# Attention of a decoder trunk on one core: the next queries' rotation before the normalising, one sum and reciprocal for a pair of heads, and low parts of outputs and late weights on GpSimd

## The chip, the cores and the metric

One NeuronCore of a Trainium2 chip runs the whole kernel. The metric is the time of one execution on the device in microseconds (us); before the change the median of three runs is 1023.88 us. Engines are named as in the profile: PE is TensorE (matrix products and transposes), DVE is VectorE, ACT is ScalarE, POOL is GpSimd, SP is SyncE, which issues loads.

## The reference, cut to what matters

A residual stream of 512 tokens and 1024 channels passes a gated convolution layer with its feed-forward layer, and then a layer of sliding-window attention with its feed-forward layer. The change touches only the attention: 16 query heads of 64 channels, 4 shared key and value heads, blocks of 128 queries that see their own and the previous 128 keys, and one learned sink per head that takes part in the softmax.

```
q = partial_rotary((rmsnorm(h) @ w_q).reshape(s, 16, 64))
scores = einsum(q, k) / 8, masked to the last 128 keys
probs = softmax(concatenate([scores, sink]))[..., :-1]
attn = einsum(probs, v) @ w_o
h = h + rmsnorm(attn)
```

## The kernel before, in words

All products are in float32 made of two parts: a tile is rounded to a high part (on ACT, `AF.Copy` into an fp32r tile) and the rest, value minus high part, is its low part (a `tensor_tensor` subtract, mostly on DVE). Three matmuls, high by low, high by high and low by high, make one product (`mm3`, L193 to L195 of the profile).

The attention handles eight pairs of heads, t = 0 to 7. It is written as rounds i = 0 to 9 of a loop, and the string `ORDER` says in which order the steps of a round are recorded; every engine then works through its own instructions in just that order. A letter is a step, a digit its part, and a minus at its end means the pair before. In round i:

- `R-` rotates the queries of pair i+1: DVE shuffles the PSUM tile `pq` into `sh` (L1261) and multiplies `pq` by the cosines into `ra` (L1263); POOL multiplies `sh` by the sines (L1267) and adds it to `ra` (L1270). Once L1263 has read it, the PSUM bank of `pq` is free again.
- `S0 S1` are the scores of pair i on PE (L1334, tiles `psc`). For the rounds in `NEXT` (0 to 4, 6 and 7) `S1` is moved right behind `S0`, and then its banks come from the four that `pq` also uses.
- `M0 M1` are mask and maxima on DVE (L1346), `E00` to `E11` the exponentials on ACT (L1362) with the sink's own exponential after each half (L1369). Half 0 is query blocks 0 and 1, half 1 is blocks 2 and 3.
- `N0 N1` normalise on DVE: for each half an addition of sums and sink (L1374), a reciprocal (L1376), and four multiplications of the exponentials (L1379, tiles `s`).
- `T0` to `T3` transpose the probabilities of pair i-1 on PE (L1391, tiles `pt`), `P` and `L` make their high and low parts (L1404 on ACT, L1408 on DVE), `W` multiplies them by the values (L1417, tiles `po`).
- `O-` joins the two halves of `po` of pair i-2 (L1426 on ACT, L1428 on DVE), `o-` splits the result into high and low part (L1436 on ACT, L1437 on DVE). The output products read these: those of pairs 0 to 3 (`Z`, `z`, tiles `pe`) from round 5 on, those of pairs 4 to 7 (tiles `pmix`) behind the loop.
- `Q0` to `Q3` project the queries of pair i+2 on PE into `pq`; `G` loads and splits the weights of pair i+3, and in rounds 5 to 8 the late output weights `rest_w` (L182 on ACT, L183 on DVE); `g` does so for the early ones; `H-` splits the rotated queries of pair i+1 (L1280 on ACT, L1281 on POOL).

Beside that the loop issues transfers on POOL's queue that add weight blocks in memory for the second feed-forward layer (L547). They are released at the ends of rounds by `sum_on`; `R-` issues half of those that wait and `H-` the rest. In the trace a round is best counted from the first instruction of `M0` on DVE, the only place where L1346 has 128 columns; rounds 1 to 5 begin at 557.8, 569.7, 583.7, 596.8 and 612.7 us.

Of the kernel before, what the change touches and what calls it, by code (L numbers as in the profile page):

```python
# [44 lines left out]

EARLY_IN, REST_IN = 2, 0
ORDER = (
    "R- S0 T0 T1 O- Q0 M0 Q1 o- Z0 P0 P1 S1 T2 T3 L0 Q2 L1 G M1 E00 E01 k H- g0 Q3 P2 P3 E10 E11 Z1 z0 W0 L2 L3 A A A N0 W1 W2 N1 W3 g1 z1"
)
NEXT = (0, 1, 2, 3, 4, 6, 7)  # L50
STEP = {
# [6 lines left out]
EARLY = 4  # L58
# [16 lines left out]
def yoco_kernel(  # L75
# [22 lines left out]
    nc = tc.nc  # L98
# [7 lines left out]
    small = ctx.enter_context(tc.tile_pool(name="small", bufs=3))  # L106
# [7 lines left out]
    def name(s):  # L114
        uid[0] += 1
        return f"{s}_{uid[0]}"
# [55 lines left out]
            h = at[1].start // S  # L172
            return self.of[h][:, at[1].start - h * S : at[1].stop - h * S]

    def split_weights(src, raw=None, slots=False):
        if raw is None:
            raw = fetch(src)
        if slots:
            hi, lo = Two("whi", F32R), Two("wlo", F32R)
            for h in range(2):  # L180
                c = slice(h * S, (h + 1) * S)
                nc.scalar.activation(hi[:, c], raw[:, c], AF.Copy)  # L182
                nc.vector.tensor_tensor(out=lo[:, c], in0=raw[:, c], in1=hi[:, c].bitcast(F32),  # L183
                                        op=ALU.subtract)
            return hi, lo
        hi = wsp.tile([P, D], F32R, tag="whi", name=name("whi"))
        lo = wsp.tile([P, D], F32R, tag="wlo", name=name("wlo"))
        nc.scalar.activation(hi, raw, AF.Copy)
        nc.vector.tensor_tensor(out=lo, in0=raw, in1=hi.bitcast(F32), op=ALU.subtract)
        return hi, lo  # L190
# [366 lines left out]
    for l in range(2):  # L557
# [3 lines left out]
        for rd, (f0, f1) in enumerate(ROUNDS[:-1]):  # L561
            k = slice(f0 // 2, f1 // 2)
# [744 lines left out]
    class Heads:  # L1307
# [44 lines left out]

        def exponents(self, half, i):
            pe, nm = self.pe[half], self.nm[half]
            if i == 0:
                se = small.tile([P, 2, 2], F32, tag="se", name=name("se"))
                rs = small.tile([P, 2, 2], F32, tag="rs", name=name("rs"))
                self.sums[half] = se, rs
            se, rs = self.sums[half]
            cc = self.spans(half)[i][1]  # L1360
            for e in range(2):
                nc.scalar.activation(  # L1362
                    pe[e][:, cc], pe[e][:, cc], AF.Exp, bias=nm[:, e, i : i + 1],
                    scale=-1.0, accum_out=rs[:, e, i : i + 1],
                )
            if i == 1:
                for e in range(2):
                    h = 2 * self.t + e
                    nc.scalar.activation(se[:, e], nm[:, e], AF.Exp, bias=snk[:, h : h + 1])  # L1369

        def normalise(self, half):
            se, rs = self.sums[half]
            pe = self.pe[half]
            nc.vector.tensor_tensor(out=se, in0=se, in1=rs, op=ALU.add)  # L1374
            rd = small.tile([P, 2, 2], F32, tag="rd", name=name("rd"))
            nc.vector.reciprocal(out=rd, in_=se)  # L1376
            for i, cc in self.spans(half):
                for e in range(2):
                    nc.vector.tensor_scalar(  # L1379
                        out=pe[e][:, cc], in0=pe[e][:, cc], scalar1=rd[:, e, i : i + 1],  # L1380
                        scalar2=None, op0=ALU.mult,
                    )
# [48 lines left out]
        def out(self):  # L1431
            if self.t < BOTH:
                hi, lo = halves("ohl", F32R)
            else:
                hi, lo = slot("ohi", F32R), slot("olo", F32R)
            nc.scalar.activation(hi, self.o, AF.Copy)  # L1436
            nc.vector.tensor_tensor(out=lo, in0=self.o, in1=hi.bitcast(F32), op=ALU.subtract)  # L1437
            at.append((hi, lo))

    class Early:  # L1440
# [17 lines left out]
    early_w, rest_w = [], []  # L1458
# [5 lines left out]
    with tc.manual_schedule(engines=ALL):  # L1464
# [20 lines left out]
        for hf in range(2):  # L1485
            c = slice(hf * 256, (hf + 1) * 256)
# [41 lines left out]
        src = [p.rearrange("p (g e d) -> p g e d", g=2, d=HD) for p in pv]  # L1528
        for j in range(NB):
            nc.scalar.activation(dst[j][:, :, 0::3], src[j], AF.Copy)  # L1530
        for j in range(NB):
            if j == 2:
                qs[0].split(nc.vector)
            nc.vector.tensor_tensor(out=dst[j][:, :, 1:3], in0=src[j],
                                    in1=dst[j][:, :, 0::3].bitcast(F32), op=ALU.subtract)

    with tc.manual_schedule(engines=ALL):
        sum_on("a0")
        for i in range(KT + 2):
# [9 lines left out]
            for c in order.split():  # L1549
# [4 lines left out]
                if c == "k":  # L1554
                    if i == 3:
                        ks.append(rope_split(rot_k, nc.gpsimd))
                    continue
                late = c.endswith("-")
                op, n = c[0], [int(d) for d in c[1:].rstrip("-")]
                t = i - late  # L1560
                if op == "g":

                    u = 2 * (t - EARLY - 1) + n[0]
                    if u in (-2, -1, 2, 3):
                        j = u + 2 if u < 0 else u
                        early_w.append(split_weights(w_o[j // 2, j % 2], slots=j >= EARLY_IN))
                    continue
                if op in "SMENTPLWOo":
                    t -= op in "TPLWOo"
                    of = hp  # L1570
                elif op in "QRH":
                    t += LEAD
                    of = qs
                elif op == "G":
                    t += LEAD + 1
                    of = qs
                    if KT <= t < KT + 4:
                        j = t - KT
                        rest_w.append(split_weights(w_o[j // 2, 2 + j % 2], slots=j >= REST_IN))
                else:  # L1580
                    t = 2 * (t - EARLY - 1) + n.pop(0)
                    of = early
# [107 lines left out]
```

## Time and profile before

| | us |
|---|---|
| median of three runs | 1023.88 |
| lowest and highest of the three | 1023.8, 1024.68 |
| the profiled execution's own time | 1024.8 |
| its span, first to last instruction | 1021.9 |
| PE busy in the span | 1005.3 |
| DVE, ACT, POOL busy | 879.1, 589.6, 190.2 |
| attention, first scores to last values product | 547.5 to 660.2 |

Times in the trace count from the first instruction. 2.9 us lie outside the span. PE shows as busy 98% of the span, so the share alone says little about where a stage loses time; the waits of PE and the rounds of the attention stage say more. A matmul's row begins when it is issued, and its end is modelled.

### The profile page before, as it was taken

To read this page: it belongs to the slowest core of one execution; us is meant where nothing else is said; L and a number is where in the kernel's file an instruction comes from. 1 tells how busy PE (TensorE), PEld (TensorE's weight loads), DVE (VectorE), ACT (ScalarE), POOL (GpSimd) and SP (SyncE) were. 2 spreads that over 40 slices of the span, in tenths; PEclk is the share of its full clock that TensorE was granted. 3 is DMA by queue.
4 is the path that set the end of the run, shared out by engine and by line. 5 is a ranking of instruction groups with operands and counts; after the bars stand their busy time and mean duration, and the time that the engine had idled before them with its cause. 6 is when DMAs were issued, how large, how long until landed. Compare 5 with 4: busy or idle time off the path is not lost.

```text
span 1021.9 us, 16136 instructions
## 1 busy us (share of the span) xinstructions
PE 1005.3 (98%) x5944; PEld 888.4 (87%) x5944; DVE 879.1 (86%) x1496; ACT 589.6 (58%) x1051; POOL 190.2 (19%) x251
## 2 busy tenths in 40 slices
PE   9999999999999999999999899999999999999997
PEld 8888888999889898998898777789998998989986
DVE  5766767899789989999879999888997899999896
ACT  6323445875655454656476678768566564645641
POOL 0443033112111111100114553221211010110001
PEclk9999999999999999999999999999999999999999
DMA  9897689559979699779405889976899676979742
GB/s 359 288 268 223 182 250 347 150 168 286 346 242 299 201 304 342 215 224 327 167 22 149 191 246 235 255 264 165 249 306 320 184 236 221 287 289 257 264 159 83
DMA packets 66575, 244.50 MB, mean 239 GB/s; under 512 B 7872, under 2 KB 8384, under 8 KB 54720
## 3 DMA queue, kind: packets, MB, share of 16 engines
q1 hardware_dynamic: 51328, 145.98, 38.4%
q0 software_dynamic: 14592, 96.48, 37.6%
q10 hardware_dynamic: 576, 1.02, 0.3%
q8 instruction: 46, 0.75, 0.3%
q14 instruction: 33, 0.27, 0.1%
HBM read 237.15 MB, written 102.76 MB: 333 GB/s over the span
## 4 chain that ended last, share of the span: by engine, by line
PE 91%; DVE 7%; ACT 2%; issue 0%; DVEq 0%; ACTq 0%
PE gx L1072 14%; PE gx L1075 7%; PE gz L195 4%; PE gz L193 4%; PE gz L194 4%; PE pcub L194 4%; PE pcub L193 4%; PE pcub L195 4%; PE px L194 4%; PE px L193 4%; PE px L195 4%; PE pmix L195 3%; PE pmix L193 3%; PE pmix L194 3%; PE gy L194 2%; PE gy L193 2%
## 5 line engine op out<-in xcount | busy, mean ns | idle before, releaser
L479 DVE TENSOR_TENSOR wlo<-raw,whi 128x1024 fp32r<-128x1024 f32 x225 | 274.7, 1225 | 53.0 <-ACT whi L478 52.8
L478 ACT ACTIVATE whi<-raw 128x1024 fp32r<-128x1024 f32 x225 | 233.7, 1051 | 100.4 <-DVE raw L466 28.8
L1072 PE MATMUL gx<-xt,whi 128*128 128x512 f32 x480 | 120.4, 393 | 0.0
L1072 PEld LDWEIGHTS gx<-xt,whi 128*128 128x128 f32 x480 | 86.2, 189 | 15.6
L547 POOL DMA_DIRECT2D hsum<-in_w_gb_dram x96 | 62.9, 734 | 152.9 <-ACT whi L478 90.0
L1034 DVE TENSOR_TENSOR st<-gx,st 128x256 f32<-128x256 f32 x200 | 78.0, 419 | 2.5 <-ACT st L1050 0.4
L1050 ACT ACTIVATE st<-gx 128x256 f32<-128x256 f32 x120 | 43.5, 380 | 62.3 <-PE gx L1075 58.6
L547 POOL DMA_DIRECT2D hsum<-hsum x32 | 25.4, 793 | 289.8 <-ACT whi L478 219.3
L1075 PEld LDWEIGHTS gx<-xt,wlo 128*128 128x128 f32 x480 | 65.5, 190 | 4.7
L1075 PE MATMUL gx<-xt,wlo 128*128 128x256 f32 x480 | 66.9, 282 | 0.0
L1086 ACT ACTIVATE gr<-gr 128x1024 f32<-128x1024 f32 x20 | 21.2, 1062 | 50.1 <-DVE gr L1034 50.1
L193 PE MATMUL px<-wlo,ahi 128*128 128x512 f32 x120 | 46.7, 389 | 0.0
L194 PE MATMUL px<-whi,ahi 128*128 128x512 f32 x120 | 46.7, 389 | 0.0
L195 PE MATMUL px<-whi,alo 128*128 128x512 f32 x120 | 46.7, 389 | 0.0
L195 PE MATMUL gz<-xhi,wlo 128*128 128x256 f32 x160 | 45.5, 284 | 0.0
L193 PE MATMUL gy<-xlo,whi 128*128 128x256 f32 x160 | 45.3, 283 | 0.0
L194 PE MATMUL gy<-xhi,whi 128*128 128x256 f32 x160 | 45.3, 283 | 0.0
L193 PE MATMUL gz<-xt,whi 128*128 128x256 f32 x160 | 45.3, 283 | 0.0
L194 PE MATMUL gz<-xt,whi 128*128 128x256 f32 x160 | 45.3, 283 | 0.0
L193 PE MATMUL gz<-xlo,whi 128*128 128x256 f32 x160 | 45.3, 283 | 0.0
L195 PE MATMUL gz<-xt,wlo 128*128 128x256 f32 x160 | 45.3, 283 | 0.0
L195 PE MATMUL gy<-xhi,wlo 128*128 128x256 f32 x160 | 45.3, 283 | 0.0
(293 smaller groups left out, 2969.5 us busy)
## 6 DMA issues: line engine op xcount, KB each, us to landing
hsum<-in_w_gb_dram POOLq DMA_DIRECT2D x96, 512.0 KB, 7.6
raw<-hsum SPq DMA_DIRECT2D x88, 512.0 KB, 8.0
raw<-in_w_gb_dram SPq DMA_DIRECT2D x60, 512.0 KB, 7.1
hsum<-in_w_dn_dram POOLq DMA_DIRECT2D x36, 512.0 KB, 8.1
raw<-in_w_dn_dram SPq DMA_DIRECT2D x32, 512.0 KB, 5.9
hsum<-hsum POOLq DMA_DIRECT2D x28, 512.0 KB, 5.7
raw<-in_w_in_dram SPq DMA_DIRECT2D x21, 512.0 KB, 7.4
hsum<-in_w_dn_dram POOLq DMA_DIRECT2D x12, 768.0 KB, 10.3
```

The source lines that it names most:

```text
L193: nc.tensor.matmul(out, whi, xlo, start=start, stop=False, **kw)
L194: nc.tensor.matmul(out, whi, xhi, start=False, stop=False, **kw)
L195: nc.tensor.matmul(out, wlo, xhi, start=False, stop=stop, **kw)
L478: self.begun = nc.scalar.activation(hi[:, :n], raw, AF.Copy)
L479: nc.vector.tensor_tensor(out=lo[:, :n], in0=raw, in1=hi[:, :n].bitcast(F32), op=ALU.subtract)
L547: nc.gpsimd.dma_start(dst, src, max_dma_last_dim=4 * 4 * S, **kw))
L1034: nc.vector.tensor_tensor(out=out, in0=a, in1=b, op=ALU.add)
L1050: nc.scalar.activation(ste, a, AF.Copy)
L1072: nc.tensor.matmul(banks[c][e], whi[:, kk], factors[p][k][2], start=opened and k == 0, stop=False, **kw)
L1075: nc.tensor.matmul(banks[c][e][:, :256], wlo[:, kk], factors[p][k][0], start=False, stop=k == 3 and p == 4, **kw)
L1086: nc.scalar.activation(kept[2], kept[2], AF.Silu)
```

## The change

Four edits:

1. `R` stands before `N0` of the same round, and is no longer at the start of the next one. It rotates pair i+2 in round i, right behind the last part of its projection. Only in round 0 there is `R-` as well, for pair 1. Since `R` comes when nothing waits to be issued, all transfers of a round go out at `H-`.
2. The sums of both halves of a pair share one tile. `N0` makes one addition and one reciprocal of 8 columns for both; `N1` only multiplies.
3. The low part of the output (`o-`) goes to POOL for pairs 0, 1, 2, 4, 5 and 6. Pairs 3 and 7, whose products follow at once, stay on DVE.
4. The low parts of three of the four late output weights (`G` in rounds 5, 6 and 7, two tiles of 512 columns each) go to POOL.

```diff
-    "... Z1 z0 W0 L2 L3 A A A N0 W1 W2 N1 W3 g1 z1"
+    "... Z1 z0 W0 L2 L3 R A A A N0 W1 W2 N1 W3 g1 z1"
...
-    def split_weights(src, raw=None, slots=False):
+    def split_weights(src, raw=None, slots=False, eng=nc.vector):
...
-                nc.vector.tensor_tensor(out=lo[:, c], in0=raw[:, c], in1=hi[:, c].bitcast(F32),
-                                        op=ALU.subtract)
+                eng.tensor_tensor(out=lo[:, c], in0=raw[:, c], in1=hi[:, c].bitcast(F32),
+                                  op=ALU.subtract)
...
         def exponents(self, half, i):
-            if i == 0:
-                se = small.tile([P, 2, 2], F32, tag="se", name=name("se"))
-                rs = small.tile([P, 2, 2], F32, tag="rs", name=name("rs"))
-                self.sums[half] = se, rs
-            se, rs = self.sums[half]
+            if half == i == 0:
+                self.sums = [small.tile([P, 2, 2, 2], F32, tag=s, name=name(s))
+                             for s in ("se", "rs")]
+            se, rs = (x[:, half] for x in self.sums)
...
         def normalise(self, half):
-            se, rs = self.sums[half]
             pe = self.pe[half]
-            nc.vector.tensor_tensor(out=se, in0=se, in1=rs, op=ALU.add)
-            rd = small.tile([P, 2, 2], F32, tag="rd", name=name("rd"))
-            nc.vector.reciprocal(out=rd, in_=se)
+            if half == 0:
+                se, rs = self.sums
+                nc.vector.tensor_tensor(out=se, in0=se, in1=rs, op=ALU.add)
+                self.rd = small.tile([P, 2, 2, 2], F32, tag="rd", name=name("rd"))
+                nc.vector.reciprocal(out=self.rd, in_=se)
+            rd = self.rd[:, half]
...
         def out(self):
-            nc.vector.tensor_tensor(out=lo, in0=self.o, in1=hi.bitcast(F32), op=ALU.subtract)
+            eng = nc.vector if self.t in (EARLY - 1, KT - 1) else nc.gpsimd
+            eng.tensor_tensor(out=lo, in0=self.o, in1=hi.bitcast(F32), op=ALU.subtract)
...
+                if c == "R-" and i:
+                    continue
...
-                        rest_w.append(split_weights(w_o[j // 2, 2 + j % 2], slots=j >= REST_IN))
+                        rest_w.append(split_weights(w_o[j // 2, 2 + j % 2], slots=j >= REST_IN,
+                                                    eng=nc.vector if j == 3 else nc.gpsimd))
```

On DVE, at the end of round 0, this stood in a row before: the last maximum, the first half's sum, reciprocal and multiplications, the second half's, and then the rotation of pair 2 (`sh`, `ra`).

```order
L1374 TENSOR_TENSOR se_5707<-se_5707,rs_5708 128x4
L1376 RECIPROCAL rd_5735<-se_5707 128x4
L1379 TENSOR_SCALAR s_5676<-s_5676,rd_5735 128x128
L1379 TENSOR_SCALAR s_5677<-s_5677,rd_5735 128x128
L1379 TENSOR_SCALAR s_5676<-s_5676,rd_5735 128x256
L1379 TENSOR_SCALAR s_5677<-s_5677,rd_5735 128x256
L1374 TENSOR_TENSOR se_5726<-se_5726,rs_5727 128x4
L1376 RECIPROCAL rd_5742<-se_5726 128x4
```

At the same place now (the rotation's `sh` and `ra` first, then one sum and one reciprocal of 8 columns, then the multiplications of half 0; those of half 1 follow):

```order
L1346 ISA nm_5700 128x1
L1261 STREAM_SHUFFLE sh_5732<-pq_5668 128x512
L1263 TENSOR_TENSOR ra_5734<-pq_5668,ctab_5215 128x512
L1374 TENSOR_TENSOR se_5707<-se_5707,rs_5708 128x8
L1376 RECIPROCAL rd_5739<-se_5707 128x8
L1380 TENSOR_SCALAR s_5676<-s_5676,rd_5739 128x128
L1380 TENSOR_SCALAR s_5677<-s_5677,rd_5739 128x128
```

The rotation, which needs the finished `pq`, now stands ahead of the normalising, and the second half's sum and reciprocal are gone.

On DVE, from the end of round 1 into round 2, this stood before: half 1's normalising, the rotation, the join of the output (`o`) and the next maxima.

```order
L1374 TENSOR_TENSOR se_5873<-se_5873,rs_5874 128x4
L1376 RECIPROCAL rd_5905<-se_5873 128x4
L1379 TENSOR_SCALAR s_5845<-s_5845,rd_5905 128x256
L1379 TENSOR_SCALAR s_5846<-s_5846,rd_5905 128x256
L1379 TENSOR_SCALAR s_5845<-s_5845,rd_5905 128x256
L1379 TENSOR_SCALAR s_5846<-s_5846,rd_5905 128x256
L1261 STREAM_SHUFFLE sh_5915<-pq_5798 128x512
L1263 TENSOR_TENSOR ra_5917<-pq_5798,ctab_5215 128x512
L1428 TENSOR_TENSOR o_5964<-po_5881,o_5964 64x512
```

Now, from the last low part of the round before (`lp`) to half 0's multiplications:

```order
L1409 TENSOR_TENSOR lp_5534<-pt_5820,lp_5533 128x2x128
L1261 STREAM_SHUFFLE sh_5882<-pq_5791 128x512
L1263 TENSOR_TENSOR ra_5884<-pq_5791,ctab_5215 128x512
L1374 TENSOR_TENSOR se_5844<-se_5844,rs_5845 128x8
L1376 RECIPROCAL rd_5889<-se_5844 128x8
L1380 TENSOR_SCALAR s_5799<-s_5799,rd_5889 128x128
```

Behind half 1's multiplications the join of the output follows at once, since the rotation is done already.

On POOL, rounds 1 and 2, before: the rotation's two steps (`sh`, `ra`), a transfer, the low part of the split queries (`rhl`), a step of the second key tile (`ra_5578`), and two transfers.

```order
L1267 TENSOR_TENSOR sh_5915<-sh_5915,stab_5216 128x512
L1270 TENSOR_TENSOR ra_5917<-ra_5917,sh_5915 128x512
L547 DMA hsum_178<-hsum_176 64x2048
L1281 TENSOR_TENSOR rhl_6033<-ra_5917,rhl_6033 128x512
L1270 TENSOR_TENSOR ra_5578<-ra_5578,sh_5576 128x512
L547 DMA hsum_180<-in_w_gb_dram 64x2048
L547 DMA hsum_181<-in_w_gb_dram 64x2048
```

Now at the same place, with the output's low part (`ohl`) in between:

```order
L1267 TENSOR_TENSOR sh_5882<-sh_5882,stab_5216 128x512
L1270 TENSOR_TENSOR ra_5884<-ra_5884,sh_5882 128x512
L1439 TENSOR_TENSOR ohl_5978<-o_5953,ohl_5978 128x512
L1281 TENSOR_TENSOR rhl_6022<-ra_5884,rhl_6022 128x512
L1270 TENSOR_TENSOR ra_5578<-ra_5578,sh_5576 128x512
L547 DMA hsum_178<-hsum_176 64x2048
L547 DMA hsum_180<-in_w_gb_dram 64x2048
L547 DMA hsum_181<-in_w_gb_dram 64x2048
```

The low part of the output is new on this engine, and the transfer that went out with the rotation now stands behind the split queries.

More of the change, by code (lines that the diff above doesn't have):

```diff
@@ L47 @@
 ORDER = (
-    "R- S0 T0 T1 O- Q0 M0 Q1 o- Z0 P0 P1 S1 T2 T3 L0 Q2 L1 G M1 E00 E01 k H- g0 Q3 P2 P3 E10 E11 Z1 z0 W0 L2 L3 A A A N0 W1 W2 N1 W3 g1 z1"
+    "R- S0 T0 T1 O- Q0 M0 Q1 o- Z0 P0 P1 S1 T2 T3 L0 Q2 L1 G M1 E00 E01 k H- g0 Q3 P2 P3 E10 E11 Z1 z0 W0 L2 L3 R A A A N0 W1 W2 N1 W3 g1 z1"
 )
```

## The prediction

> **What bounds the kernel now.** I read the page first, then who TensorE (PE) waited for over the whole run, then the attention stage by rounds, then single rows of all engines there. Page and waits of PE (us in total, times, longest):
>
> ```profile
> PE 1005.3 (98%) x5944; PEld 888.4 (87%) x5944; DVE 879.1 (86%) x1496; ACT 589.6 (58%) x1051; POOL 190.2 (19%) x251
> PE psc L1334 <- DVE ra L1263: 5.2, 3, 2.0
> ```
>
> Nearly all of PE's waiting is one thing: three times the scores wait for `ra`, the rotation's read of the projected queries, which frees their PSUM bank. The other lasting loss is the clock. Stretches of the run (us; PE, PEld, DVE, ACT, POOL busy; granted clock): first two of half clock, then rounds 2, 3 and 4.
>
> ```profile
> 568.96:572.37 3.41, 3.41 (x18) 2.99 (x15) 3.35 (x13) 2.00 (x4) 2.23 (x3) 0.50 1.10 370
> 596.27:599.68 3.41, 3.41 (x17) 2.88 (x14) 3.38 (x12) 2.27 (x4) 3.33 (x5) 0.50 0.26 24
> 569.70:583.70 14.00, 12.66 (x81) 11.03 (x82) 13.06 (x39) 9.70 (x29) 7.49 (x8) 0.90 0.81 180
> 583.70:596.80 13.10, 11.08 (x78) 9.43 (x77) 12.68 (x39) 9.99 (x30) 6.92 (x8) 0.98 0.81 196
> 596.80:612.70 15.90, 15.90 (x91) 13.77 (x91) 14.80 (x42) 11.59 (x31) 7.50 (x10) 0.91 0.84 267
> ```
>
> Rounds 2 and 3 are bound by DVE, which is busy 13.06 of 14.00 and 12.68 of 13.10 us, while PE has idle time; in round 4 PE is busy throughout. The waits of PE, in its timeline:
>
> ```profile
> 568.43 0.38 PE L1334 MATMUL psc<-rlo,rhl 64*128 64x256 f32 x1 [1.84 <-DVE ra L1263]
> 582.43 0.38 PE L1334 MATMUL psc<-rlo,rhl 64*128 64x256 f32 x1 [1.34 <-DVE ra L1263]
> 595.55 0.38 PE L1334 MATMUL psc<-rlo,rhl 64*128 64x256 f32 x1 [2.02 <-DVE ra L1263]
> ```
>
> The gaps of 1.84 and 2.02 were followed by 3.41 us at half clock, that of 1.34 was not. Each such stretch does half of its work, so it costs 1.7 us where PE is the bound: 5.2 + 3.4 = 8.6 us is what the stage loses here, and the most that freeing this bank could bring.
>
> The Trainium skill ("TensorE: Matmul & The Clock Gate", the rules for kernel authors) lets the clock fall after gaps above about 3 us; the trace differs, with gaps of about 2. By that page alone the first two gaps would have cost no clock.
>
> **What the rotation's move gains and costs.** Round 3 on DVE, then ACT, then POOL:
>
> ```profile
> 585.08 0.69 DVE L1437 TENSOR_TENSOR ohl<-o,ohl 128x512 fp32r<-128x512 f32 x1
> 585.68 1.28 DVE L1408 TENSOR_TENSOR plo<-pt,phi 128x512 fp32r<-128x512 f32 x2
> ...
> 590.89 0.68 DVE L1374 TENSOR_TENSOR se<-se,rs 128x4 f32<-128x4 f32 x1
> 591.61 0.18 DVE L1376 RECIPROCAL rd<-se 128x4 f32<-128x4 f32 x1
> 591.82 1.01 DVE L1379 TENSOR_SCALAR s<-s,rd 128x128 f32<-128x128 f32 x4
> 592.74 0.15 DVE L1374 TENSOR_TENSOR se<-se,rs 128x4 f32<-128x4 f32 x1
> 592.93 0.18 DVE L1376 RECIPROCAL rd<-se 128x4 f32<-128x4 f32 x1
> 593.14 1.14 DVE L1379 TENSOR_SCALAR s<-s,rd 128x256 f32<-128x256 f32 x4
> 594.21 0.72 DVE L1261 STREAM_SHUFFLE sh<-pq 128x512 f32<-128x512 f32 x1
> 594.83 0.67 DVE L1263 TENSOR_TENSOR ra<-pq,ctab 128x512 f32<-128x512 f32 x1
> 595.42 1.40 DVE L1428 TENSOR_TENSOR o<-po,o 64x512 f32<-64x512 f32 x2
> 596.85 0.35 DVE L1346 CUSTOM_DVE_ANT_0 s<-psc,mask,nsnk 128x128 f32<-128x128 f32 x1
> ```
>
> ```profile
> 583.72 0.63 ACT L1436 ACTIVATE ohl<-o 128x512 fp32r<-128x512 f32 x1 [2.52 <-DVE o L1428]
> 592.04 0.48 ACT L1369 ACTIVATE se<-nm,snk 128x2 f32<-128x2 f32 x2
> ```
>
> ```profile
> 590.26 1.29 POOL L1281 TENSOR_TENSOR rhl<-ra,rhl 128x512 fp32r<-128x512 f32 x1
> 595.01 1.28 POOL L1267 TENSOR_TENSOR sh<-sh,stab 128x512 f32<-128x512 f32 x1 [2.34 <-DVE sh L1261]
> 596.38 1.27 POOL L1270 TENSOR_TENSOR ra<-ra,sh 128x512 f32<-128x512 f32 x1
> ```
>
> From start to start: sum 0.19 (592.93 - 592.74), reciprocal 0.21, multiplications 0.92 (592.74 - 591.82) and 1.07 (594.21 - 593.14), rotation 1.21 (595.42 - 594.21), join 1.43 (596.85 - 595.42), output's low part 0.60 (585.68 - 585.08).
>
> Gain: `ra` comes 0.40 + 0.92 + 1.07 + 0.40 = 2.8 us or more earlier against the normalising, more than any of the three waits. They go.
>
> Cost one: the merged sum waits for the second half's sinks. ACT works from 583.72 to 592.04 + 0.48 = 592.52 without an idle row, 8.80 us from the join's end; the old first sum needed only the first half and started at 590.89. What queues behind it on DVE: both normalisings, then the join, which starts ACT's next chain. A round of rounds 2 and 3 so becomes 8.80 + 0.19 + 0.21 + 0.92 + 1.07 + 1.43 = 12.6 us, whatever else leaves DVE: the 0.60 of the low part and the 0.40 of the second sum lie inside ACT's 8.8 us and bring nothing beyond that. Round 2: 14.0 to 12.6, -1.4. Round 3: 13.1 to 12.6, -0.5. Round 4 has two more weight splits on DVE, and I price it by DVE: 15.9 less 0.60, 0.40 and 0.3 of delays like that of 590.89, -1.3.
>
> Cost two: POOL's two rotation steps (1.28 and 1.27) used to run beside the join and the maxima, which read PSUM. Now they meet the normalising. The sum of 590.89 took 0.68 instead of 0.15 and ended, at 591.57, just when POOL's 590.26 + 1.29 = 591.55 did: a sum with two SBUF inputs is held by a POOL operation under way. No row shows POOL's multiplication against L1379. Bounds: 0 (not held) and 1.28 for each POOL step that is under way when a multiplication wants to start. The nearest rows, of the convolution:
>
> ```profile
> 37.61 1.51 DVE L762 TENSOR_SCALAR cut<-cut,gt 128x512 f32<-128x512 f32 x1
> 55.67 0.49 DVE L762 TENSOR_SCALAR cut<-cut,gt 128x512 f32<-128x512 f32 x1 [1.19 <-POOL cut L759]
> ```
>
> The same operation took 1.51 beside POOL's work and 0.49 elsewhere, so this kind can be held. I take held, where POOL started first; once the eight multiplications run, I take POOL to wait for them.
>
> The Trainium skill says it outright ("SBUF — State Buffer", Who interferes with whom): a DVE operation in a 2-port mode, `tensor_scalar` among them, and a GpSimd operation exclude each other, and the second to issue waits for all of the first. The 1.51 row agrees; by that rule POOL's steps cost up to 2.6 us a round where the order falls badly, and the rows decide how often it does.
>
> The opening, round 0, pays both. DVE, PE and ACT:
>
> ```profile
> 553.69 0.15 DVE L1374 TENSOR_TENSOR se<-se,rs 128x4 f32<-128x4 f32 x1
> 554.43 0.39 PE L195 MATMUL pq<-xhi,wlo 128*128 128x512 f32 x1
> 556.37 1.09 PE L1391 MATMUL pt<-ident,s 128*128 128x128 f32 x8
> 557.77 0.34 DVE L1346 CUSTOM_DVE_ANT_0 s<-psc,mask,nsnk 128x128 f32<-128x128 f32 x1
> 554.57 0.47 ACT L1369 ACTIVATE se<-nm,snk 128x2 f32<-128x2 f32 x2
> ```
>
> DVE, free at 553.69, now waits for `pq` until 554.43 + 0.39 = 554.82: 1.2 us with normalising and transposes queued behind. Rotation until 556.1; POOL's `sh` runs 0.8 after its start (595.01 - 594.21) to 557.0, and holds the sum 0.9; POOL's `ra` then runs to 558.4 and holds the multiplications 1.0. They end at 559.4 and 560.4, where round 1 began at 557.77: +2.7 (1.2 + 0.9 + 1.0 - 0.4). PE, which had no gap at 556.37, stands still 3.0 us, and its clock halves. Round 1 I therefore take at the 12.6 of the later ones, against 569.7 - 557.8 = 11.9: +0.7. POOL's later rotation steps cost 0 by this reading: the ACT wait covers the held sum.
>
> DVE is then at 2.7 + 0.7 - 1.4 - 0.5 - 1.3 = +0.2 at the start of round 5. PE (three rows), DVE and ACT in the later rounds:
>
> ```profile
> 608.05 1.09 PE L1391 MATMUL pt<-ident,s 128*128 128x128 f32 x8
> 614.82 0.49 PE L195 MATMUL pe<-whi,ohl 128*128 128x512 f32 x1 [0.43 <-DVE ohl L1437]
> 654.62 1.04 PE L1391 MATMUL pt<-ident,s 128*128 128x128 f32 x6 [0.87 <-DVE plo L1408]
> 635.06 0.15 DVE L1374 TENSOR_TENSOR se<-se,rs 128x4 f32<-128x4 f32 x1
> 635.33 0.48 ACT L1369 ACTIVATE se<-nm,snk 128x2 f32<-128x2 f32 x2
> ```
>
> From 608.05 PE is the bound, and those transposes had no wait. Between half 0's normalising and round 5 stand 1.07, a weight split of about 1.1 and 1.43 on DVE, so half 0 is now ready at 612.7 + 0.2 - 3.6 = 609.3: PE 1.2 late. It recovers the 0.43 of 614.82, since `ohl` (pair 3, still on DVE) is ready by then.
>
> **The low parts on POOL** free DVE of 6 x 0.60 for outputs and 6 x 0.60 for weights of the same shape, 7.2 us in all, and cost POOL 12 x 1.29 = 15.5 us. In rounds 2 to 4 ACT's chain hides the gain, in rounds 5 to 7 PE's and ACT's work: in round 6 the old sum began at 635.06, the merged one waits for 635.33 + 0.48 = 635.81 however free DVE is, +0.75 against the 0.40 saved. In round 8 the low part stood right ahead of `plo`, for which PE waited 0.87: of that 0.6 goes. I count +0.4 and -0.6. The readers of the low parts on POOL are products a round or more later, except pair 6's, which the products behind the loop read: the transposes of 654.62 and the last pair's products with the values still lie between, which covers 1.29 instead of 0.69. If a transfer held POOL up there, PE would wait as long; I count 0.
>
> **The transfers** that left at `R-` leave at `H-`, half a round later, on POOL behind the split queries. They fill memory that the second feed-forward layer reads, behind the whole loop, and POOL's rotation steps, which now follow them, have a reader half a round on: 0. If POOL ran out of time, `rhl` would be late for the scores of the round after; POOL is busy 7 us of 13 to 16 in rounds 2 to 4 and gets 1.3 more.
>
> The sum: +1.2 - 0.4 + 0.4 - 0.6 = +0.6 us on the execution's own 1024.8, so 1025.4. That execution was 0.9 above the median of 1023.88; against the median the forecast is 1024.5.
>
> **Rivals.** *Faster:* POOL's steps do not hold the multiplications, and PE's pause in the opening is too short to halve the clock. Then the opening costs 2.7 - 1.0 = 1.7, round 1 nothing more, and DVE stands at 1.7 - 1.4 - 0.5 - 1.3 = -1.5 at round 5, 1.7 less than above; nor need the later waits of PE, spread over a round, halve the clock once more, another 1.7 that had been paid in round 4. That gives 0.6 - 1.7 - 1.7 = -2.8: 1021.1. For it: no row shows a multiplication of L1379 held. Against it: the 1.51, and that 1.84 us sufficed for the clock.
>
> *Slower:* POOL gets between the eight multiplications. It decides from the point where the rotation's `sh` becomes ready while they run, that is, where POOL's transfers or split queries delay it by some 1.5 us, as the new order at `H-` makes likely. Each time one step of 1.28 is added to a round whose length DVE and ACT set in a loop; in rounds 1 to 3 once each, +3.8, so 0.6 + 3.8 = +4.4: 1028.3. For it: the normalising and both POOL steps now stand side by side in six rounds. Against it: the multiplications follow without a gap (four take 1.14 and the next row starts 1.07 after the first), so POOL may find no free moment.
>
> *Nothing in the transposes:* all of DVE's changes hide behind PE, which is busy for 98%. The rows of rounds 2 and 3, with PE idle for 1.3 and 2.0 us, speak against it; it would give 0, 1023.9, and falls in with the forecast.
>
> **How the numbers follow.** 0.2%, about what a measurement of this kernel can tell from no change, is 2 us. I give the forecast, with the third rival, 0.42, the faster rival 0.30, the slower one 0.28. The forecast's own range is 1022.6 to 1026.4: the opening's held parts (1.9) may be missing or the clock (1.7) fall once more. The range for 8 in 10 takes in most of both other cases: 1020.6 to 1028.2. Of the forecast's 0.42, about 0.06 lies beyond 2 us on either side; of the rivals some 0.05 each lies within. So faster 0.31, same 0.40, slower 0.29.
>
> **What would show it.** Right: no wait of PE for `ra` L1263; L1374 starting when ACT's second sinks end, rounds 2 and 3 of about 12.6 us; a gap of 2 to 3 us on PE near 556 followed by half clock; PE waits that name L1379. L1379 at more than 0.35 beside POOL's L1267 or L1270 shows that it is held, a stretched row in the middle of the eight shows the slower rival. Wrong: rounds 2 to 4 below 12 us, so that ACT's chain did not bound them, or PE waiting for POOL.

## The result and the profile after

The changed kernel takes 1041.66 us (median of four runs, 1040.12 to 1043.6), the kernel before took 1023.84 us beside it: ratio 1.0174, 95% interval 1.0155 to 1.0193, so 17.8 us slower. The forecast was 1024.5, and even the slower rival, 1028.3, is far below.

The profiled execution took 1041.2 us; its span is 1039.4 where it was 1021.9. Busy time, from the page:

```profile
PE 1010.5 (97%) x5944; PEld 890.6 (86%) x5944; DVE 882.2 (85%) x1468; ACT 589.4 (57%) x1051; POOL 205.1 (20%) x263
```

Whom PE waited for (us in total, times, longest):

```profile
PE pt L1392 <- DVE s L1380: 12.2, 8, 2.9
PE xt L338 <- ACT xn L327: 4.1, 1, 4.1
```

The waits for `ra` are gone, as meant. In their place PE waits 12.2 us for the normalised `s`, and 4.1 us once for `xn`, the normalised input of the next layer, a wait behind the attention that did not exist before. In the span's growth of 17.5 us, 5.2 are PE's busy time (1010.5 - 1005.3), which is the same work at a lower clock, and 12.3 its idle time. Apart from the run's last microseconds there are now five stretches at half clock instead of two; three of them (us; PE, PEld, DVE, ACT, POOL busy; granted clock):

```profile
574.09:577.50 3.41, 3.41 (x9) 2.63 (x10) 3.38 (x12) 2.84 (x7) 1.29 (x1) 0.50 0.88 339
587.75:591.16 3.41, 3.26 (x11) 2.42 (x12) 3.35 (x12) 0.48 (x1) 0.00 (x0) 0.50 1.01 209
...
696.97:700.38 3.41, 3.28 (x16) 3.28 (x17) 2.80 (x5) 1.50 (x4) 0.29 (x1) 0.50 0.61 235
```

**In the loop.** The rounds 1 to 4, counted as before, by the same view:

```profile
559.93:574.65 14.72, 11.93 (x80) 9.77 (x79) 14.59 (x37) 8.46 (x28) 7.83 (x8) 0.98 0.57 109
574.65:590.68 16.03, 13.81 (x79) 11.27 (x79) 13.77 (x36) 9.46 (x29) 8.77 (x8) 0.82 0.73 187
590.68:605.76 15.08, 11.88 (x80) 9.89 (x79) 13.81 (x36) 9.98 (x30) 8.22 (x8) 0.95 0.55 150
605.76:622.92 17.16, 14.30 (x74) 11.90 (x73) 16.27 (x38) 11.36 (x31) 8.75 (x10) 0.83 0.65 159
```

They were 11.9, 14.0, 13.1 and 15.9 us; now 14.72, 16.03, 15.08 and 17.16. The normalising in round 1, on DVE, then the same time on POOL:

```profile
566.87 0.67 DVE L1263 TENSOR_TENSOR ra<-pq,ctab 128x512 f32<-128x512 f32 x1
567.46 0.91 DVE L1374 TENSOR_TENSOR se<-se,rs 128x8 f32<-128x8 f32 x1
...
568.64 4.67 DVE L1380 TENSOR_SCALAR s<-s,rd 128x128 f32<-128x128 f32 x8
```

```profile
566.69 2.65 POOL L547 DMA_DIRECT2D hsum<-in_w_gb_dram  x4
568.80 1.83 POOL L1267 TENSOR_TENSOR sh<-sh,stab 128x512 f32<-128x512 f32 x1
570.71 1.39 POOL L1270 TENSOR_TENSOR ra<-ra,sh 128x512 f32<-128x512 f32 x1
```

Four transfer issues stand ahead of `sh` on POOL, so it begins 0.16 us after the first multiplication. From there POOL and DVE take turns: the eight multiplications take 4.67 us. Narrower cuts of the same timeline, the first two multiplications and two of the next:

```profile
568.64 2.08 DVE L1380 TENSOR_SCALAR s<-s,rd 128x128 f32<-128x128 f32 x2
570.64 1.61 DVE L1380 TENSOR_SCALAR s<-s,rd 128x256 f32<-128x256 f32 x2
```

One of the first pair ends at 570.72, right behind `sh` (568.80 + 1.83 = 570.63), and one of the second at 572.25, right behind `ra` (570.71 + 1.39 = 572.10). Each step of POOL got in between two multiplications, and the next multiplication waited for all of it. Round 2 shows the other order that occurs; the rows of DVE, then those of POOL:

```profile
584.46 1.71 DVE L1374 TENSOR_TENSOR se<-se,rs 128x8 f32<-128x8 f32 x1
586.44 2.89 DVE L1380 TENSOR_SCALAR s<-s,rd 128x128 f32<-128x128 f32 x8
```

```profile
584.05 2.09 POOL L1267 TENSOR_TENSOR sh<-sh,stab 128x512 f32<-128x512 f32 x1
586.21 1.26 POOL L1270 TENSOR_TENSOR ra<-ra,sh 128x512 f32<-128x512 f32 x1
```

`sh` is under way when the sum wants to start, and the sum ends with it (586.17 and 586.14); `ra` begins beside the reciprocal and holds the first multiplication. Over all rounds (line, form, number, then busy us and mean ns):

```profile
L1380 DVE TENSOR_SCALAR s<-s,rd 128x256 f32<-128x256 f32 (+1 forms) x64 | 24.5, 454 | 0.3
L1374 DVE TENSOR_TENSOR se<-se,rs 128x8 f32<-128x8 f32 x8 | 7.0, 878 | 1.8 <-ACT se L1368 1.8
```

The sums have a mean of 878 ns, where the shortest of before, of 4 columns each, took 147.

**Behind the loop.** The first product of `pmix` starts at 671.81 instead of 660.16, 11.7 us later; the other 5.9 us are lost after it. POOL, then ACT, then PE:

```profile
688.14 0.83 POOL L547 DMA_DIRECT2D hsum<-in_w_dn_dram  x1 [6.51 <-DMA hsum<-in_w_dn_dram]
690.03 0.79 POOL L547 DMA_DIRECT2D hsum<-in_w_dn_dram  x1 [1.06 <-DMA hsum<-in_w_dn_dram]
690.57 0.85 POOL L322 TENSOR_TENSOR ur<-uv,mhalf 128x1 f32<-128x1 f32 x1
691.11 0.83 POOL L300 TENSOR_TENSOR ur<-uv,mhalf 128x1 f32<-128x1 f32 x1
691.46 1.15 ACT L327 ACTIVATE xn<-h,ur 128x1024 f32<-128x1024 f32 x1 [5.75 <-POOL ur L322]
697.10 2.18 PE L338 MATMUL xt<-ident,xn 128*128 128x128 f32 x9 [4.11 <-ACT xn L327]
```

The residual update needs two power steps of one column on POOL (`ur`, L300 and L322) for each block of 128 tokens. The L322 of the first block stands in POOL's queue behind two transfer issues that wait until earlier transfers have landed; it is 6 us late, and PE pauses 4.11 us, with half clock behind it (696.97).

### The profile page after: what moved, and what is told of

The parts are those of the page before. It is cut to its first block, busy times and chain, and to the rows that moved or that the text cites. A ratio compares the mean times of both kernels' runs of the same rounds, so it can differ in the third digit from the quotient of the medians.

```text
span 1039.4 us, 16128 instructions
## 1 busy us (share of the span) xinstructions
PE 1010.5 (97%) x5944; PEld 890.6 (86%) x5944; DVE 882.2 (85%) x1468; ACT 589.4 (57%) x1051; POOL 205.1 (20%) x263
## 4 chain that ended last, share of the span: by engine, by line
PE 88%; DVE 4%; DMA 3%; ACT 2%; issue 2%; POOL 1%; DVEq 0%; SPq 0%; POOLq 0%; ACTq 0%
PE gx L1072 14%; PE gx L1075 7%; PE gz L195 4%; PE gz L193 4%; PE gz L194 4%; PE pcub L194 4%; PE pcub L195 4%; PE pcub L193 4%; PE px L193 4%; PE px L194 3%; PE px L195 3%; PE pmix L195 2%; PE pmix L193 2%; PE pmix L194 2%; PE gy L195 2%; PE gy L194 2%
## 5 line engine op out<-in xcount | busy, mean ns | idle before, releaser
L479 DVE TENSOR_TENSOR wlo<-raw,whi 128x1024 fp32r<-128x1024 f32 x225 | 274.5, 1224 | 52.9 <-ACT whi L478 52.7
```

What stands on the lines that cost most here:

```text
L479: nc.vector.tensor_tensor(out=lo[:, :n], in0=raw, in1=hi[:, :n].bitcast(F32), op=ALU.subtract)
```

## Experiments

**First theory:** POOL's two rotation steps, now beside the normalising, hold DVE's sum and multiplications, and the transfers, now issued late, hold the residual update. **Rival:** the merged sum, which waits for ACT's second sinks, delays the transposes. **Second rival:** the low parts on POOL cost its time. Loop is the time from the first score to the first product of `pmix`, rest from there to the end of the span; waits for `s` are PE's. These three come from one profiled execution of each kernel, the ratio from all its runs beside the kernel before.

| kernel | ratio, 95% interval | loop | rest | waits for `s` |
|---|---|---|---|---|
| before | 1 | 112.7 | 361.7 | 0.2 |
| changed | 1.0174 (1.0155 to 1.0193) | 124.5 | 367.6 | 12.2 |
| e4 move only | 1.0155 (1.0140 to 1.0170) | 128.6 | 361.7 | 10.2 |
| e3 rotation back | 1.0032 (1.0019 to 1.0044) | 114.5 | 362.7 | 0.9 |
| e6 low parts only | 1.0012 (1.0003 to 1.0021) | 111.3 | 363.3 | 0.2 |
| e7 merged sum only | 1.0038 (1.0025 to 1.0050) | 114.7 | 361.7 | 0.2 |
| e1 POOL's steps later | 1.0131 (1.0116 to 1.0147) | 119.9 | 367.3 | 5.7 |
| e10 both mended | 0.9995 (0.9986 to 1.0003) | 109.7 | 362.9 | 1.7 |
| e9 both mended, move only | 0.9985 (0.9976 to 0.9994) | 111.0 | 361.7 | 1.5 |
| e5 transfers mended | 1.0108 (1.0091 to 1.0124) | 121.8 | 363.0 | 9.5 |
| e14 POOL's steps mended | 1.0036 (1.0023 to 1.0048) | 110.6 | 366.3 | 1.7 |
| e12 late transfers only | 1.0018 (1.0005 to 1.0031) | 112.5 | 361.7 | 0.2 |
| e11 mended, pair 6 on DVE | 0.9982 (0.9974 to 0.9991) | 110.7 | 361.6 | 1.7 |
| e13 the same, two sums | 0.9985 (0.9977 to 0.9994) | 111.3 | 361.7 | 1.1 |

### Which part of the change costs

The move alone, on the kernel before:

```diff
-    "... W0 L2 L3 A A A N0 W1 W2 N1 W3 g1 z1"
+    "... W0 L2 L3 R A A A N0 W1 W2 N1 W3 g1 z1"
...
+                if c == "R-" and i:
+                    continue
```

> The kernel before with the move of the rotation (and of the first half of the transfers) alone: two sums and reciprocals for each pair, all low parts on VectorE. First theory: nearly all of the loss is there, 1034 to 1042 us, normalising rows of VectorE stretched beside GpSimd's steps. Rival (merged sum): 1020 to 1026. Second rival (low parts on GpSimd): no wait for the residual update, and about 1024 to 1030.

Measured 1039.25 us. Its sums and multiplications (normalising of half 0 and half 1 apart):

```profile
L1379 DVE TENSOR_SCALAR s<-s,rd 128x256 f32<-128x256 f32 (+1 forms) x64 | 22.4, 412 | 0.6
L1374 DVE TENSOR_TENSOR se<-se,rs 128x4 f32<-128x4 f32 x16 | 11.1, 694 | 0.0
```

Together 33.5 us, where the same 80 instructions take 19.7 (17.2 and 2.5) in e9 below, whose rotation steps on POOL stand behind them. The move alone brings nearly all of the loss. PE does not wait for `xn` here: the two issues ahead of `ur` stand at 687.72 and 689.64, about where they stand in the changed kernel, while this loop ends 4.2 us later.

The reverse, the changed kernel with the order of before and its `R-` in every round:

> The changed kernel with the rotation, and with it the first half of the transfers, back at the start of the next round; the merged sum and reciprocal and the low parts on GpSimd stay. First theory (the move alone costs): TensorE's waits for s go, those for ra come back (about 5 us), 1021 to 1026 us. Rival (merged sum): 1030 or more, TensorE waits for s. Second rival (the low parts take GpSimd's time and make the transfers late): the residual update at 690 us still waits for GpSimd's transfers, about 1030.

Measured 1026.9 us: the waits for `s` are gone (0.9), those for `ra` are back (6.7). Of 17.8 us some 14.5 go with the move, 3.3 stay. The two rivals can speak for no more than these 3.3. They are told apart by putting the low parts alone and the merged sum alone on the kernel before, with the edits 3 and 4, and 2, of the change:

> The kernel before with the low parts of outputs and of late output weights on GpSimd alone; two sums, rotation at the start of the round. The kernel with merged sum and low parts was 3.5 us slower than before; this tells which of the two it is. If the merged sum's waits for ScalarE (1.30, 0.37, 1.52, 1.59, 0.68, 1.58 us on VectorE there) are the cost, as I think: within 1.5 us of before. If the low parts on GpSimd are the cost (they delay the output behind the loop, 0.87 us of a wait of TensorE for ohi there): 1025 to 1027.

> The kernel before with one sum and one reciprocal for each head pair alone. If the merged sum is the cost: 1025 to 1027 us, VectorE idle ahead of the sum until ScalarE's second sinks, TensorE's waits for ra longer than before's 5.2 us. If not: within 1.5 us of before.

Measured 1024.8 and 1027.79 us. Without the move, the merged sum is the cost (3.9 us), as DVE's wait for ACT's sink in round 3 of e7 shows:

```profile
594.15 0.17 DVE L1374 TENSOR_TENSOR se<-se,rs 128x8 f32<-128x8 f32 x1 [1.59 <-ACT se L1368]
```

The low parts shorten the loop by 1.4 us and lose 1.6 behind it.

### Where POOL's rotation steps stand

In e1 they are put behind the low part of an output in POOL's queue, by a step `r-` of their own; `B` is the part on DVE.

```diff
-    "R- S0 T0 T1 O- Q0 M0 Q1 o- Z0 ... L2 L3 R A A A N0 ..."
+    "R- S0 T0 T1 O- Q0 M0 Q1 o- r- Z0 ... L2 L3 B A A A N0 ..."
```

> The changed kernel, but GpSimd's two steps of the rotation (sh, ra) stand behind the low part of an output in GpSimd's queue, so that they run in the next round and no longer beside the normalising; VectorE's order, the merged sum, the low parts on GpSimd and the place of the transfers stay. GpSimd has nothing to wait for there in rounds 0 and 4, so these two stay as they are. First theory (GpSimd's steps beside the normalising hold the sum and the multiplications): normalising, 5.85, 4.87, 4.90 and 4.10 us in rounds 1, 2, 3 and 5, comes down to 2.5 there, about 9.7 us less on VectorE; TensorE's waits for s go from 12.2 us to under 5; 1031 to 1034 us, and if the late residual update at 690 us goes as well, 1026. Rival (the merged sum, which waits for ScalarE's second sinks, keeps the transposes waiting): 1040 to 1042, waits for s as long as now.

Measured 1036.74 us, less gain than expected. In rounds 0 and 4 the hold stays, as foreseen. Where the steps are out of the way, the normalising is what it should be, as here in round 1:

```profile
569.47 0.15 DVE L1381 TENSOR_TENSOR se<-se,rs 128x8 f32<-128x8 f32 x1
569.89 2.06 DVE L1387 TENSOR_SCALAR s<-s,rd 128x128 f32<-128x128 f32 x8
```

The rounds 1 to 3 take 39.2 us instead of 45.8. But in the later rounds POOL's steps now meet another operation of DVE that reads SBUF alone, the split of a weight. POOL's queue, pushed back by the rotation steps, still holds its own split and that of the queries there. DVE, then POOL:

```profile
639.06 3.50 DVE L183 TENSOR_TENSOR wlo<-raw,whi 128x512 fp32r<-128x512 f32 x2 [1.61 <-ACT whi L182]
645.82 1.29 DVE L183 TENSOR_TENSOR wlo<-raw,whi 128x512 fp32r<-128x512 f32 x2
```

```profile
637.80 2.54 POOL L183 TENSOR_TENSOR wlo<-raw,whi 128x512 fp32r<-128x512 f32 x2
```

Two such subtractions take 3.50 us beside POOL's work and 1.29 alone. And the residual update still waits (3.8 us of PE).

So in e9 and e10 POOL's steps are tied to the end of the normalising, by one column that POOL reads from the output of the last multiplication. They then run beside the join and the maxima, which read PSUM, where they ran before the change. The transfers are issued at the start of a round again.

```diff
+        def begin(self):
+            self.begun = rope_begin(self.ps)
+
+        def finish(self):
+            last = hp[self.t - LEAD].pe[1][1][:, 2 * P - 1 : 2 * P]
+            seen = small.tile([P, 1], F32, tag="seen", name=name("seen"))
+            nc.gpsimd.tensor_tensor(out=seen, in0=last, in1=last, op=ALU.mult)
+            rope_turn(self.begun[0], nc.gpsimd)
+            self.rot = rope_add(*self.begun, nc.gpsimd)
...
-    "... L2 L3 R A A A N0 W1 W2 N1 W3 g1 z1"
+    "... L2 L3 B A A A N0 W1 W2 N1 r W3 g1 z1"
...
                 if c == "R-" and i:
+                    if i <= KT:
+                        issue(len(issues) // 2)
                     continue
```

> The changed kernel with GpSimd's two rotation steps kept behind the normalising in the same way, and transfers at the start of the round; merged sum and low parts on GpSimd as changed. First theory: sum and eight multiplications 2.5 us in all rounds, also 0 and 4, which the first experiment could not reach; no residual update waits; loop at 112 to 116 us, 1022 to 1027, above the same with two sums by the cost of the merged sum. Rival: 1030 or more, with TensorE waiting for s although no multiplication is stretched.

> The kernel before with the rotation's reads by VectorE ahead of the normalising, and GpSimd's two steps kept behind the normalising by a one-column GpSimd operation that reads the last multiplication's output and so waits for it; transfers at the start of the round, two sums, low parts on VectorE. So the bank is free early and GpSimd's steps lie where they lay before, beside the join and the maxima. First theory (only GpSimd's steps beside the normalising, and the late transfers, cost): no waits for ra, normalising 2.5 us, the loop 3 to 8 us shorter than the kernel before's 112.7 us: 1015 to 1021. Rival (the rotation's 1.2 us ahead of the normalising on VectorE delays the transposes by as much in every round, GpSimd or not): the waits for s stay at 1 us and more in most rounds, 1024 to 1031.

Measured: e10 1023.36 us, the whole loss gone; e9 1022.27 us, less gain than expected. In e10, the group rows, then the rounds 1 to 4:

```profile
L1390 DVE TENSOR_SCALAR s<-s,rd 128x256 f32<-128x256 f32 (+1 forms) x64 | 16.5, 332 | 0.3
L1384 DVE TENSOR_TENSOR se<-se,rs 128x8 f32<-128x8 f32 x8 | 1.3, 161 | 1.9 <-ACT se L1378 1.9
```

```profile
558.48:569.93 11.45, 11.37 (x81) 9.75 (x80) 11.25 (x37) 8.47 (x28) 9.41 (x11) 1.00 0.75 166
569.93:582.10 12.17, 11.38 (x80) 9.38 (x79) 11.86 (x37) 9.47 (x30) 9.06 (x10) 1.00 0.84 209
582.10:594.80 12.70, 11.75 (x80) 9.42 (x79) 11.87 (x37) 10.00 (x31) 8.45 (x9) 1.00 0.86 221
594.80:609.51 14.71, 13.11 (x78) 10.47 (x77) 13.83 (x38) 11.37 (x31) 10.58 (x12) 1.00 0.83 244
```

The same 72 instructions take 17.8 us instead of 31.5. So the hold cost DVE 13.7 us in six rounds. Only the place of POOL's steps, with the one-column step that fixes it, differs between e5 (next) and e10: 121.8 and 109.7 us for the loop. The first theory's main half is shown.

By the ratios, mending the steps alone brings 14.1 of the 17.8 us (e14 below), the transfers alone 6.8 (e5), both together 18.3 (e10).

### The transfers

e5 is the changed kernel with the last four lines of that diff alone:

> The changed kernel, with half of a round's transfers issued at the start of the round again, behind GpSimd's rotation steps, as in the kernel before. First theory, with the late transfers as its second half: sh no longer stands behind four transfer issues, so it starts right behind the shuffle; normalising comes to about 4.1 us in rounds 1 to 4, as in rounds 0 and 5 now (4 us less in all), and the transfers are issued early enough that the residual update at 690 us does not wait (5.8 us less): 1030 to 1034 us. If the transfers' place does not matter: 1040 to 1042.

Measured 1035.09 us. The residual update no longer waits; POOL's two issues no longer wait for a landing, and the power step behind them waits for DVE alone:

```profile
680.23 0.94 POOL L300 TENSOR_TENSOR ur<-uv,mhalf 128x1 f32<-128x1 f32 x1 [8.76 <-DVE uv L296]
681.13 1.66 POOL L547 DMA_DIRECT2D hsum<-in_w_dn_dram  x2
684.00 0.55 POOL L322 TENSOR_TENSOR ur<-uv,mhalf 128x1 f32<-128x1 f32 x1 [1.22 <-DVE uv L318]
```

But the hold did not shrink by the expected 4 us: sums and multiplications take 30.0 (8.2 and 21.8) instead of 31.5. In none of the six rounds does POOL now get in between the multiplications: the sum ends with `sh`, and the first multiplication with `ra`. Round 1, DVE, then POOL:

```profile
568.53 1.50 DVE L1374 TENSOR_TENSOR se<-se,rs 128x8 f32<-128x8 f32 x1
570.31 2.96 DVE L1380 TENSOR_SCALAR s<-s,rd 128x128 f32<-128x128 f32 x8
```

```profile
568.69 1.30 POOL L1267 TENSOR_TENSOR sh<-sh,stab 128x512 f32<-128x512 f32 x1
570.08 1.26 POOL L1270 TENSOR_TENSOR ra<-ra,sh 128x512 f32<-128x512 f32 x1
```

That `sh` starts late does not matter much; that it stands beside the normalising does.

e14 is the other half, e10 without those four lines, and e12 is the kernel before with all of a round's transfers at `H-` from round 1 on:

```diff
-                if op in "RH" and i <= KT:
+                if (op == "H" or (op == "R" and not i)) and i <= KT:
```

> The changed kernel with GpSimd's two rotation steps kept behind the normalising, and all transfers of a round still issued behind the split queries, as changed. With both mended it was 1023.4 us, with the transfers alone mended 1035.1. First theory (two costs, each of its own place): the loop at 110 to 112 us as with both mended, normalising 2.5 us in every round, and behind the loop a residual update that waits for GpSimd's transfers, TensorE idle 4 us or more near 680 us: 1028 to 1032. If the transfers were late only because the loop's rounds were stretched: 1023 to 1025, no such wait.

> The kernel before, with all transfers of a round issued behind the split queries instead of half of them at the round's start; nothing else. The prediction counted this move at 0. Theory: the last transfers come some 7 us later against the end of the loop, GpSimd's power step of the residual update (needed 12.6 us after the loop) stands behind them, TensorE waits some 4 us for the normalised input and its clock halves once: 1028 to 1031. If the prediction's 0 was right: 1023 to 1025.

Measured 1026.87 us for e14, a little less than expected, with the wait of PE behind the loop (2.74 us, and half clock at 683.09). Before it on POOL:

```profile
673.73 0.83 POOL L547 DMA_DIRECT2D hsum<-in_w_dn_dram  x1 [5.09 <-DMA hsum<-in_w_dn_dram]
...
676.14 0.85 POOL L322 TENSOR_TENSOR ur<-uv,mhalf 128x1 f32<-128x1 f32 x1
```

e12 took 1025.46 us, but its runs spread from 1023.07 to 1029.35. In its profiled execution (1023.33 us) the same issues stand at 671.58 and 673.68 and `ur` at 674.23, and PE does not wait. It lies near the lower end of that spread, and no profile shows where the longer executions lose time.

So the late transfers alone cost 1.8 us by the median (0.5 to 3.2 by the interval), less than I expected and more than the 0 of the prediction; with the low parts on POOL ahead of them in its queue they cost 4.2 us (e14 against e10, 1.0036 - 0.9995). The first of the two issues comes 11.7 us after the first product of `pmix` in e12's profile, 14.9 us after it in e14's; it is 11.7 in e4 too, which has the low parts on DVE, and 16.3 in the changed kernel. That the low parts' waits for ACT's high parts in the queue make this difference is argued from the order, not shown by a run of its own.

### Pair 6's low part, and two sums

e10 still lost 0.93 us behind the loop, in a wait for `ohi`. There DVE's three weight splits of the next layer took longer than in e9, where pair 6's low part is on DVE. e10, then e9:

```profile
655.75 4.60 DVE L425 TENSOR_TENSOR wlo<-raw,whi 128x1024 fp32r<-128x1024 f32 x3 [0.68 <-ACT whi L420]
662.38 0.50 PE L193 MATMUL pmix<-wlo,ohi 128*128 128x512 f32 x1 [0.93 <-ACT ohi L1447]
```

```profile
657.55 3.50 DVE L425 TENSOR_TENSOR wlo<-raw,whi 128x1024 fp32r<-128x1024 f32 x3 [0.69 <-ACT whi L420]
```

```diff
-            eng = nc.vector if self.t in (EARLY - 1, KT - 1) else nc.gpsimd
+            eng = nc.vector if self.t in (EARLY - 1, KT - 2, KT - 1) else nc.gpsimd
```

> The changed kernel with both mended, and the low part of pair 6's output back on VectorE: on GpSimd it ran beside VectorE's three weight splits of the next layer, which took 4.60 us instead of 3.50, and TensorE waited 0.93 us for ohi behind the loop. Theory: that wait goes and nothing comes in its place, 1 us less than the 1023.4 with pair 6 on GpSimd: 1021.9 to 1022.9. If it was another engine's delay: 1023 to 1024.

> As the kernel with both mended and pair 6 on VectorE, but with two sums and reciprocals for each pair as before, so that the first half's normalising need not wait for ScalarE's second sinks. By the merged sum's price without the move (4 us: 1027.8 against 1023.9) it would be 1019 to 1020.5. By VectorE's rounds with the rotation ahead of the sum, which waited for ScalarE only 0.2 to 0.7 us, the two are equal within 1 us: 1021.5 to 1022.9; I take this.

Measured 1021.71 and 1022.28 us. The wait is gone and the rest is back at 361.6. The two sums bring nothing here: with the rotation ahead of it, the one sum of e11 waits for ACT in four of the eight rounds, 0.2 to 0.7 us each. The gain from e10 to e11 is shown in that wait alone: the intervals of the two overlap, and e11's profiled loop is 1.0 us longer (110.7 against 109.7). Both kernels are faster than the one before, e11 by 1.8 us (0.9 to 2.7), and so is e9; among the three the intervals do not tell a best one.

## Why the prediction was wrong

**The step that failed** is POOL's price in the rounds behind the opening: "POOL's later rotation steps cost 0 by this reading: the ACT wait covers the held sum." In round 0 the prediction had `sh` hold the sum and `ra` the multiplications; the same came in rounds 2, 4 and 5 of the changed kernel, and in all six rounds of e5. There was no cover: the sum followed the rotation on DVE at once, or waited for ACT 0.34 us (round 3), where the hold was 2.4 us. The prediction counted 1.9 us of hold, in the opening alone; the runs show 13.7 in six rounds (31.5 - 17.8). The other half of the price, "once the eight multiplications run, I take POOL to wait for them", failed as well: in round 1 both steps of POOL got in between the multiplications, in round 3 `ra` did. But this changed little, as e5 shows. Both steps of POOL meet the normalising because DVE's part of the rotation, which releases them, now ends where the sum begins. The gap was on record: "No row shows POOL's multiplication against L1379", with bounds of 0 and 1.28 for each step. Twelve steps at the upper bound are 15.4 us, near what came; for rounds 1 to 5 the lower end was taken. The row of 1.51, from which it took the multiplications to be held, was weak ground: beside it stood transfer issues until 38.77, and POOL's next tensor step began at 38.79, 0.33 us before the row's end.

The Trainium skill ("SBUF — State Buffer", Who interferes with whom) says that the issue order decides who blocks, and that the other is blocked for the whole instruction. The trace agrees: `sh` of 568.80 and the multiplication behind it end at 570.63 and 570.72. The instruction meant there is one multiplication, not the row of eight for which the prediction took it.

**The slower rival** had POOL between the multiplications because transfers delay it, one step in each of three rounds, 3.8 us on top of the opening's 1.9. That came in rounds 1 and 3. But without the delay (e5) POOL no longer got in between, and the hold stayed; so the rival's reason is not the cause, and its size was less than half. Nor is the forecast's clock loss the one that came: the opening's gap was 2.00 us, not 3.0, and no half clock followed, which was luck (see the last section); the later rounds' gaps did it.

**The transfers** were counted 0, because the memory they fill is read late. That is true of the data. What was not followed is POOL's queue behind them: an issue that waits for a landing holds whatever follows it, here `ur`. Behind the loop the changed kernel lost 5.9 us. With the transfers early 4.6 of them come back (e5, 367.6 to 363.0), where a wait for `ohi` shows instead (1.2 us of PE); from e14 to e10 it is 4.2 us in all.

**Pair 6's low part** was counted 0 because a reader was far off; what it cost was not a late reader but DVE's weight splits beside it, 1.1 us (4.60 against 3.50), of which 0.93 reached PE.

**What held.** The waits for `ra` went. The opening, counted in parts, came nearly as said: a wait for `pq` of 1.10 (1.2 predicted), a sum of 0.90 that takes 0.15 unheld (0.75 more, 0.9 predicted), multiplications of 2.90 for 2.06 (0.84 more, 1.0 predicted). Once the hold is gone, the rounds have the length that was forecast: e10's rounds 2, 3 and 4 take 12.17, 12.70 and 14.71 us, predicted were 12.6, 12.6 and 14.6. That ACT's chain sets it is not shown: in e9 no sum waits for ACT, and rounds 2 and 3 take 12.31 and 12.67 us all the same; in e10 DVE is busy 11.86 of the 12.17.

**What is worth less than it looked** is the loss of before. The prediction put it at 8.6 us: 5.2 of waits and 3.4 of clock. e9 and e11 have neither, and are 1.5 and 1.8 us faster. In e11 PE's waits have moved to others in the same loop:

```profile
PE pt L1402 <- DVE s L1390: 1.7, 3, 0.9
PE pq L193 <- DVE o L1439: 1.6, 2, 0.8
PE po L1428 <- DVE plo L1419: 1.2, 2, 0.8
PE po L1428 <- DVE nm L1356: 1.0, 1, 1.0
```

These are 5.5 us, and PE's idle time in the whole span is 16.3 us where it was 16.6. Two half-clock stretches fewer left PE's busy time only 1.8 us shorter (1003.5 against 1005.3), not 3.4. Why they cost so little is open.

## What to carry to other kernels

Before a step is moved on one engine, look at what its completion releases on another, and which operation that will then stand beside: here GpSimd's tensor steps were free beside VectorE's reads of PSUM (a join took 0.67 to 0.70 us in the kernel before, with a step beside it or not) and cost up to their full length beside operations that read and write SBUF alone (a multiplication of 0.28 us took 1.12 to 1.88). Where a price lies between "not held" and "held for all of it" and no row shows it, multiply the upper end by the number of times it occurs before choosing. And a queue that also issues transfers is no place for a small step that others wait for, unless the transfers ahead of it surely need not wait; that holds above all when they are issued later.

## What the runs showed of the hardware

GpSimd does not wait for the end of a row of VectorE operations: in rounds 1 and 3 of the changed kernel it got in between multiplications of 0.28 to 0.34 us that follow each other without a gap, and the next of them took 1.35 to 1.88 us.

The clock can fall after several short gaps as after one long: in the changed kernel PE idled 1.17, 0.83 and 0.79 us between 569.9 and 573.9, each gap shorter than the 1.34 that was harmless before, and half clock followed at 574.09. A single gap of 2.00 us at 556.3 was not followed by it, one of 2.07 at 585.6 was.

What decides is shown by the places of the stretches. In each profile they start a whole multiple of 3.413 us apart (in the changed kernel those of 587.75, 604.81, 618.47 and 696.97 come 4, 9, 13 and 36 times 3.413 us after that of 574.09), and what counts is PE's idle time between two such points. The three short gaps leave 1.98 us idle from 570.68 to 574.09. The gap of 2.00 us is parted by the point at 557.03, and the fuller interval has 1.40 us idle; in e4 a gap of the same 2.00 us (556.38 to 558.38) lies whole between two points, and half clock followed at 558.71. Worked out from PE's rows and the granted clock of the 14 profiles, from 30 to 1005 us: of the intervals that ran at full clock, all 20 with 1.75 us idle or more were followed by half clock, and none with less than 1.45; between these it went both ways. So a gap of about 2 us costs the clock or not by where it falls, which nobody chose here.

The sum of 567.46 took 0.91 us with only transfer issues beside it on GpSimd (566.69 to 569.34; the tensor step before them had ended at 566.76). What held it is open. Issues as such did not hold VectorE elsewhere: in the kernel before, 78 weight splits (L479, two inputs in SBUF) had only issues beside them, and all took 1.21 to 1.23 us.
